# Layer norm of the convolution module: later weight splits, one more row sum on TensorE, and two edits of emission order

## The chip, the cores and the metric

The kernel runs on one core of a Trainium2 chip. The metric is the device time of one execution in microseconds (us); the time of a kernel is the median over its runs. The kernel before takes 2760.52 us, the median of three runs from 2760.06 to 2764.99. The engines are called PE (TensorE), DVE (VectorE), ACT (ScalarE), POOL (GpSimd) and SP (SyncE, which here only issues transfers).

## The reference, cut to what matters

One inference step of a decoder trunk with two layers. The first begins with a Conformer convolution module over 1074 token columns (1040 prompt columns with 16 learned tokens and a little padding, 32 sample columns) of width 1024:

```
def conv_module(x, prefix, w_pw1, b_pw1, w_dw, b_dw, ln_g, ln_b, w_pw2, b_pw2):
    a, g = jnp.split(x @ w_pw1 + b_pw1, 2, axis=-1)
    u = a * jax.nn.sigmoid(g)
    y, tail = causal_dwconv(u, prefix, w_dw)          # 31 taps
    y = jax.nn.silu(layer_norm(y + b_dw, ln_g, ln_b))
    return y @ w_pw2 + b_pw2, tail
```

All matrix products are wanted at float32 accuracy. After this module come a convolutional feed-forward layer, latent attention for the prompt and for eight sample sequences that read a paged cache, and a second feed-forward layer. Only the end of the convolution module and the layer norm behind it are touched by the change.

## The kernel before, in words

Activations lie transposed: the 1024 features are eight tiles of 128 partitions, and a tile has 1074 columns (T0). A float32 operand is split into a high part, rounded by ACT (`split`, L135), and a low part, the rest, by DVE or POOL (L136); a product is three matmuls (high by high, high by low, low by high).

The convolution module (`conv_phase`) goes over the eight feature tiles, c = 0 to 7. Each iteration makes both halves of the first product for its tile (the gemm at L419, with the gate at L402 and L403), then the 31-tap convolution (`conv31`), which leaves the tile y. The taps are multiply-adds on DVE (L523). For the last tile, c = 7, one of the three partial convolutions is done by PE instead: sixteen diagonal matrices of 128 by 128, written by ACT (L395) into two buffers of the pool of raw weights (name `raw`), are multiplied with the shifted sums (L532). A running sum of the tiles y, `total`, is kept by POOL (L446) for the mean of the layer norm.

Between these steps the kernel works off an independent list of pieces, the norms of the cached keys (`cache_norms`): three matmuls into a PSUM tile `pk` (L654), then squares by ACT, either as one square `sq` (L658) which POOL adds up pairwise (L663), or as eight small ones `qq` with an accumulator each (L669). `pk` has two buffers.

`layer_norm` does the following in turn. PE sums `total` and the last tile over the features with a matrix of ones (L573); that is mu. ACT copies it to `m` (L580). DVE subtracts it from tiles 0 to 5 (L585), POOL from tiles 6 and 7 (L583). ACT squares each tile (L589, into buffers named `xl`). The squares of tiles 0, 1 and 2 go to PE directly; those of tiles 4 to 7 are first added on DVE into that of tile 3 (L593). PE makes the sums of the rows, nine matmuls of two columns for each operand that it is given (`add_rows`, L300; the trace counts each of these float32 matmuls as two records). Then DVE computes the reciprocal root (L255 to L260) and PE and ACT spread it over the partitions (L268 to L274). The tiles are scaled (L458), go through SiLU (L460) and are split, and the second product `pw2` begins: the gemm of L175, whose first two weight tiles are loaded and split beforehand (`ahead`, through `weight`, L156).

Each engine works strictly in its own order of instructions. That order is not the order of the code: a scheduler places every instruction by its own estimate of times, with priorities (`high_priority`), except where `manual_schedule` fixes PE's or SP's order. `follow(late, early)` ties one instruction behind another in the order, without a wait. The pool `wp` holds two buffers each for `raw`, `wh` and `wl`; a transfer into a `raw` buffer has to wait until the last reader of that buffer is done, and which of the two buffers a load gets is decided together with the order. All these loads are issued by SP, in order.

Of the kernel before, what the change touches and what calls it, by code (L numbers as in the profile page):

```python
# [9 lines left out]
F32 = mybir.dt.float32  # L10
# [63 lines left out]
HALVE = 16  # L74
HEADS = (0, 1, 2, 3)
SUBS = (6, 7)
# [42 lines left out]
class Prog:  # L119
# [214 lines left out]
    def conv_phase(self):  # L334
# [3 lines left out]
        with ExitStack() as es:  # L338
# [44 lines left out]
            for c in range(KD):  # L383
# [6 lines left out]
                if c == KD - 1:  # L390
                    for half in range(2):
                        d = self.wp.tile([128, 1024], F32, name="raw")
                        for j in range(8):
                            diag.append(d[:, 128 * j:128 * j + 128])
                            nc.scalar.activation(diag[-1], self.cst("ident"), AF.Copy, scale=wsum[:, c, 8 * half + j:8 * half + j + 1])  # L395

# [14 lines left out]
                else:  # L411
                    ch, cnt = T0 // 3, 0
                    for t in range(3):
                        ps = [p.tile([128, 1, 512], F32, name="g")[:, :, :ch] for p in (ga, gg)]
                        with self.manual():
                            for w, p in zip(ws, ps):
                                for k in range(KD):
                                    for i, (x, m) in enumerate(((w[0], xh), (w[0], xl), (w[1], xh))):
                                        y = nc.tensor.matmul(p[:, 0], x[:, k * 128:(k + 1) * 128], m[k][:, t * ch:t * ch + ch],  # L419
                                                             start=k == 0 and i == 0, stop=k == KD - 1 and i == 2)  # L420
                                        self.follow(y, self.wedge)
                                        self.wedge = []
                                        cnt += 1
                                        if EVERY and cnt % EVERY == EVERY // 2:
                                            next(self.fill, None)
                        self.wedge = [y]
                        glu(*ps, t)
# [3 lines left out]
                with self.tc.high_priority(PRIO):  # L431
# [12 lines left out]
                    nc.gpsimd.memset(y[:, 0:2], 0.0)  # L444
                    if 0 < c < KD - 1:
                        nc.gpsimd.tensor_tensor(out=total, in0=total if c > 1 else ys[0], in1=y, op=ALU.add)  # L446
                ys.append(y)
# [20 lines left out]
            self.help = 0  # L468
            ahead = [self.weight(a["pw2"][ot], 1024) for ot in range(2)]
            with self.manual():  # L470
# [94 lines left out]
    def layer_norm(self, ys, total):  # L565
# [12 lines left out]
        with self.tc.high_priority(PRIO):  # L578
# [8 lines left out]
            for k in range(KD):  # L587
# [4 lines left out]
                else:  # L592
                    nc.vector.tensor_tensor(out=qs[-1], in0=qs[-1], in1=q, op=ALU.add)  # L593
            self.add_rows(t, qs, T0)
        self.groups(FILL2)
# [1296 lines left out]
```

## Time and profile before

| | before |
|---|---|
| median of three runs | 2760.52 us (2760.06 to 2764.99) |
| the profiled execution, its own time | 2764.3 us |
| its span, first to last instruction | 2762.4 us |
| mean granted TensorE clock | 0.981 of full |
| PE busy | 2652.8 us, 96% of the span |
| DVE, ACT, POOL busy | 1878.0, 1356.2, 711.0 us |

A row of the timeline gives the start in us, the length, the engine, the line, the operation with the tile written and the tiles read, the shape and the count; in brackets stands how long the engine sat idle before it and what ended the wait. Several equal instructions in a row are merged into one row. Lines are those of the kernel before.

### The profile page before, as it was taken

What the parts mean: (1) busy time and instruction counts of PE and PEld (TensorE: products, weight loads), DVE (VectorE), ACT (ScalarE), POOL (GpSimd) and SP (SyncE); (2) the same over time, 40 slices, a digit from 0 to 9 for tenths busy, and PEclk for the clock granted to TensorE, in tenths of its full rate; (3) what the DMA queues carried; (4) which work ended last, traced back from release to release, by engine and by line L of the source; (5) the groups of instructions that cost most, each with busy time, mean ns of one, the idle gap of its engine ahead of it and who ended that gap; (6) DMA issues with size and microseconds to landing.
All of it is one profiled execution on the core that took longest, in us unless ns stands there. A gap on an engine that the chain in (4) does not pass through costs nothing.

```text
span 2762.4 us, 46569 instructions
## 1 busy us (share of the span) xinstructions
PE 2652.8 (96%) x16966; PEld 2448.0 (89%) x16966; DVE 1878.0 (68%) x3485; ACT 1356.2 (49%) x3701; POOL 711.0 (26%) x1019
## 2 busy tenths in 40 slices
PE   7999997999999999999889999999999999999999
PEld 6888876999999999999767776667999999999999
DVE  8899986578888875135677767676377777775232
ACT  6777775345444553023555555566245454453010
POOL 1567663024333330001111212110023333330000
PEclk9999997999999999999989999999999999999999
DMA  4211101502322236123100001267402222227122
GB/s 142 57 41 55 39 29 42 173 32 87 95 88 94 80 105 238 47 81 107 35 11 18 26 24 32 80 199 261 152 24 89 80 77 85 80 97 244 41 87 76
DMA packets 127769, 238.24 MB, mean 86 GB/s; under 512 B 39778, under 2 KB 81140, under 8 KB 127412
## 3 DMA queue, kind: packets, MB, share of 16 engines
q1 hardware_dynamic: 103828, 200.82, 22.6%
q0 software_dynamic: 9600, 32.36, 3.1%
q10 hardware_dynamic: 14112, 2.09, 0.5%
q8 instruction: 133, 2.18, 0.3%
q14 instruction: 96, 0.79, 0.1%
HBM read 183.90 MB, written 51.31 MB: 85 GB/s over the span
## 4 chain that ended last, share of the span: by engine, by line
PE 85%; DVE 6%; ACT 5%; DMA 2%; issue 2%; POOL 0%; SPq 0%; ACTq 0%; DVEq 0%; POOLq 0%
PE ps L796 30%; PE ps L175 22%; PE pk L654 5%; PE v L1337 5%; PE g L419 4%; PE ps L845 3%; PE p L151 2%; PE ps L197 2%; PE ps L1013 1%; PE po L1651 1%; PE p L1347 1%; PE p L1350 1%; PE p L1349 1%; PE s L1307 1%; PE sn L151 1%
## 5 line engine op out<-in xcount | busy, mean ns | idle before, releaser
L135 ACT ACTIVATE wh<-raw 128x512 fp32r<-128x512 f32 (+2 forms) x256 | 191.1, 749 | 542.0 <-PE ps L175 338.5
L136 DVE TENSOR_TENSOR wl<-raw,wh 128x512 fp32r<-128x512 f32 (+2 forms) x244 | 201.5, 829 | 111.4 <-ACT wh L135 109.2
L942 DVE TENSOR_TENSOR x<-ps,x 128x1074 f32<-128x1074 f32 (+1 forms) x48 | 61.0, 1270 | 293.1 <-PE ps L175 293.1
L766 DVE SCALAR_TENSOR_TENSOR c<-ub,c,c 128x1040 f32<-128x1040 f32 (+1 forms) x176 | 225.1, 1312 | 28.6 <-ACT c L763 27.6
L761 POOL COPY sb<-ub 128x32 f32<-128x32 f32 x88 | 88.8, 1011 | 400.9 <-DVE ub L807 363.2
L669 ACT ACTIVATE qq<-pk 128x64 f32<-128x64 f32 x736 | 158.1, 243 | 67.6 <-PE pk L654 67.5
L1337 PE MATMUL v<-pf,vf 128*128 128x512 f32 (+4 forms) x448 | 176.6, 478 | 10.0 <-ACT pf L1354 9.7
L663 POOL TENSOR_TENSOR sq<-sq 128x256 f32<-128x256 f32 (+4 forms) x229 | 140.2, 623 | 102.6 <-ACT sq L658 95.6
L175 PE MATMUL ps<-xh,wh 128*128 128x358 f32 (+1 forms) x672 | 148.3, 329 | 9.1 <-ACT xh L135 5.9
L1354 ACT ACTIVATE pf<-p 128x512 f32<-128x512 f32 (+4 forms) x224 | 99.0, 451 | 118.1 <-DVE p L1352 98.1
L669 ACT ACTIVATION_READ_ACCUMULATOR qq<-pk 128x1 f32 x736 | 153.9, 227 | 0.0
L523 DVE SCALAR_TENSOR_TENSOR a<-u,c,a 128x512 f32<-128x512 f32 x216 | 150.1, 745 | 4.9 <-ACT a L516 4.9
L175 PE MATMUL ps<-xh,wl 128*128 128x358 f32 (+1 forms) x672 | 147.6, 328 | 0.0
L175 PE MATMUL ps<-xl,wh 128*128 128x358 f32 (+1 forms) x672 | 147.4, 327 | 0.1
L175 PE MATMUL ps<-al,wh 128*128 128x358 f32 (+1 forms) x672 | 147.2, 327 | 0.0
L175 PE MATMUL ps<-ah,wl 128*128 128x358 f32 (+1 forms) x672 | 146.5, 326 | 0.0
L175 PE MATMUL ps<-ah,wh 128*128 128x358 f32 (+1 forms) x672 | 146.2, 326 | 0.0
L654 PE MATMUL pk<-ukh,ch 128*128 128x512 f32 x256 | 115.5, 452 | 25.6 <-ACT ch L135 13.4
L763 ACT ACTIVATE c<-ub,c 128x1074 f32<-128x1074 f32 (+1 forms) x88 | 101.3, 1185 | 59.7 <-DVE ub L807 46.8
L175 PEld LDWEIGHTS ps<-xh,wh 128*128 128x128 f32 x672 | 117.5, 191 | 12.7 <-ACT xh L135 6.8
L658 ACT ACTIVATE sq<-pk 128x512 f32<-128x512 f32 x164 | 99.8, 613 | 50.8 <-PE pk L654 48.5
L135 ACT ACTIVATE wh<-s 128x512 fp32r<-128x512 f32 x120 | 75.7, 631 | 94.9 <-PE ps L796 88.3
(599 smaller groups left out, 9100.4 us busy)
## 6 DMA issues: line engine op xcount, KB each, us to landing
raw<-wup SPq DMA_DIRECT2D x88, 512.0 KB, 3.5
pg<-ctn SPq DMA_DIRECT2D x128, 192.0 KB, 3.8
raw<-wdn SPq DMA_DIRECT2D x32, 448.0 KB, 3.3
raw<-pw SPq DMA_DIRECT2D x24, 512.0 KB, 3.9
d_a<-c POOLq DMA_DIRECT2D x22, 537.0 KB, 3.5
raw<-d_a SPq DMA_DIRECT2D x22, 537.0 KB, 5.2
d_a<-c POOLq DMA_DIRECT2D x22, 531.0 KB, 3.1
raw<-d_a SPq DMA_DIRECT2D x22, 531.0 KB, 5.3
```

Source lines behind the costliest of these rows:

```text
L135: return (nc.scalar.activation(h, src, AF.Copy), (eng or nc.vector).tensor_tensor(out=l, in0=src, in1=h.bitcast(F32), op=ALU.subtract))
L136: (eng or nc.vector).tensor_tensor(out=l, in0=src, in1=h.bitcast(F32), op=ALU.subtract))
L175: nc.tensor.matmul(p[:, c, :ch], s[:, k * 128:(k + 1) * 128], m[k][:, off + c * ch:off + (c + 1) * ch], start=k == 0 and i == 0, stop=k == ...
L419: y = nc.tensor.matmul(p[:, 0], x[:, k * 128:(k + 1) * 128], m[k][:, t * ch:t * ch + ch], start=k == 0 and i == 0, stop=k == KD - 1 and i ...
L523: nc.vector.scalar_tensor_tensor(out=p[:, :ND] if j == n - 1 else acc, in0=x[:, j:j + ND], scalar=w[:, j:j + 1], in1=to if j == 1 else acc ...
L654: x = nc.tensor.matmul(ps, s[:, j, :], m[:, 512 * c:512 * c + 512], start=i == 0, stop=i == 2)
L663: nc.gpsimd.tensor_tensor(out=to, in0=v[:, :, :n], in1=v[:, :, n:2 * n], op=ALU.add)
L669: nc.scalar.activation(q, ps[:, 64 * h:64 * h + 64], AF.Square, accum_out=ss[:, p, 8 * c + h:8 * c + h + 1])
L763: x = nc.scalar.activation(c, ub, AF.Copy, scale=wd[:, t, 2:3])
L766: nc.vector.scalar_tensor_tensor(out=c[:, 2:pe], in0=ub[:, tap:tap + pe - 2], scalar=wd[:, t, tap:tap + 1], in1=c[:, 2:pe], op0=ALU.mult, ...
L796: nc.tensor.matmul(ps, w[:, s], m[:, lo:hi], start=first and k == 0 and i == 0, stop=k == KD // 2 - 1 and i == 2, skip_group_check=True)
L1337: nc.tensor.matmul(o[:, at_:], vf[:m, b, c], p[:m, :512 - at_], start=b == 0, stop=last)
```

## The change

Four edits. The diagonal matrices of tile 7 are no longer emitted in a block ahead of the gemm but one at each of the points in the gemm's loop where a piece of the cache work is emitted. The running sum adds a tile one iteration later (`ys[c - 1]` in iteration c), outside the priority block. The low parts of the first two `pw2` weights are tied behind `self.summed`, the last addition of squares on DVE. And the square of tile 7 is given to PE as an operand of its own instead of being added on DVE: five operands go to the row sums instead of four, in the order 0, 1, 2, 7, 3.

```
-HEADS = (0, 1, 2, 3)
+HEADS = (0, 1, 2, 3, 7)
...
-                    for half in range(2):
-                        d = self.wp.tile([128, 1024], F32, name="raw")
-                        for j in range(8):
-                            diag.append(d[:, 128 * j:128 * j + 128])
-                            nc.scalar.activation(diag[-1], self.cst("ident"), AF.Copy, scale=wsum[:, c, 8 * half + j:8 * half + j + 1])
+                    ds = [self.wp.tile([128, 1024], F32, name="raw") for _ in range(2)]
+                    diag = [ds[j // 8][:, 128 * (j % 8):128 * (j % 8) + 128] for j in range(16)]
+                made = 0
...
                                             next(self.fill, None)
+                                            if made < len(diag):
+                                                nc.scalar.activation(diag[made], self.cst("ident"), AF.Copy, scale=wsum[:, c, made:made + 1])
+                                                made += 1
...
-                    if 0 < c < KD - 1:
-                        nc.gpsimd.tensor_tensor(out=total, in0=total if c > 1 else ys[0], in1=y, op=ALU.add)
+                if c > 1:
+                    nc.gpsimd.tensor_tensor(out=total, in0=total if c > 2 else ys[0], in1=ys[c - 1], op=ALU.add)
...
-            ahead = [self.weight(a["pw2"][ot], 1024) for ot in range(2)]
+            ahead = []
+            for ot in range(2):
+                ahead.append(self.weight(a["pw2"][ot], 1024))
+                self.follow(self.last[1], [self.summed])
...
-                    nc.vector.tensor_tensor(out=qs[-1], in0=qs[-1], in1=q, op=ALU.add)
-            self.add_rows(t, qs, T0)
+                    self.summed = nc.vector.tensor_tensor(out=qs[3], in0=qs[3], in1=q, op=ALU.add)
+            self.add_rows(t, [qs[i] for i in (0, 1, 2, 4, 3)], T0)
```

What this makes of the engines' orders is shown at three places, all between the end of tile 7's convolution and the row sums. The number behind a name tells buffers apart.

SP, the loads of the second product's weights. `raw_6233` of before and `raw_6241` of the change hold the first `pw2` tile, `raw_6239` and `raw_6247` the second, the other two the third and fourth; in brackets are the engines that a transfer waits for. Before:

```order
L156 DMA raw_6233<-pw2 128x1024 [waits DMAHW7_49,PE_49]
...
L156 DMA raw_6239<-pw2 128x1024 [waits DMAHW7_49,DMAHW4_49,DVE_49]
L156 DMA raw_6493<-pw2 128x1024 [waits DMAHW5_49,PE_49]
L156 DMA raw_6660<-pw2 128x1024 [waits DMAHW6_49,DMAHW4_49,DVE_49]
L479 DMA xr_6479<-x0 128x1074
```

And in the change:

```order
L156 DMA raw_6241<-pw2 128x1024 [waits DMAHW7_49,PE_49]
...
L156 DMA raw_6247<-pw2 128x1024 [waits DMAHW4_49,PE_49]
L156 DMA raw_6501<-pw2 128x1024 [waits DMAHW5_49,DMAHW7_49,DVE_49,Activation_49]
L156 DMA raw_6668<-pw2 128x1024 [waits DMAHW4_49,DMAHW6_49,DVE_49,Activation_49]
L483 DMA xr_6487<-x0 128x1074
```

The second weight tile went, before, into the buffer of the first one, once DVE had made that one's low part; now it goes into the other buffer, whose last reader is PE's sixteenth diagonal matmul.

DVE, from the last taps of tile 7 to the reciprocal root (`x7` is the tile that `conv31` finishes, `xl3` the sum of squares). Before:

```order
L136 TENSOR_TENSOR wl_6236<-raw_6233,wh_6235 128x1024
L523 SCALAR_TENSOR_TENSOR fa_5675<-u_5067,c1_58,a1_5919 128x512
...
L541 TENSOR_TENSOR x7_5674<-g_5678,fa_5675 128x512
L542 TENSOR_TENSOR x7_5674<-fb_5676,fa_5675 128x8
L136 TENSOR_TENSOR wl_6242<-raw_6239,wh_6241 128x1024
L585 SCALAR_TENSOR_TENSOR x0_939<-ps_5982,x0_939 128x1074
...
L593 TENSOR_TENSOR xl3_6050<-xl3_6050,xl6_6058 128x1074
L593 TENSOR_TENSOR xl3_6050<-xl3_6050,xl7_6061 128x1074
L255 TENSOR_SCALAR nr_v_6152<-ps_6033 128x9
```

And in the change:

```order
L527 SCALAR_TENSOR_TENSOR fa_5674<-u_5066,c1_58,a1_5918 128x512
...
L546 TENSOR_TENSOR x7_5673<-fb_5675,fa_5674 128x8
L545 TENSOR_TENSOR x7_5673<-g_5677,fa_5674 128x512
L589 SCALAR_TENSOR_TENSOR x0_939<-ps_5982,x0_939 128x1074
...
L597 TENSOR_TENSOR xl3_6050<-xl3_6050,xl6_6058 128x1074
L136 TENSOR_TENSOR wl_6244<-raw_6241,wh_6243 128x1024
L136 TENSOR_TENSOR wl_6250<-raw_6247,wh_6249 128x1024
L255 TENSOR_SCALAR nr_v_6160<-ps_6033 128x9
```

Both low parts moved behind the additions, and the fourth addition is gone.

ACT, from the second weight's high part to the squares (`qq` and `sq` belong to the cache work, `xl0` is the square of tile 0). Before:

```order
L135 ACTIVATE wh_6241<-raw_6239 128x1024
L669 ACTIVATE qq_6013,ss_135<-pk_6009 128x64
...
L658 ACTIVATE sq_6107<-pk_6103 128x512
L580 ACTIVATE m_6034<-ps_5982 128x1074
L658 ACTIVATE sq_6119<-pk_6115 128x512
L658 ACTIVATE sq_6131<-pk_6127 128x512
L589 ACTIVATE xl0_6044<-x0_939 128x1074
L658 ACTIVATE sq_6143<-pk_6139 128x512
L589 ACTIVATE xl1_6046<-x1_1612 128x1074
L589 ACTIVATE xl6_6058<-x6_4982 128x1074
L589 ACTIVATE xl2_6048<-x2_2286 128x1074
```

And in the change:

```order
L135 ACTIVATE wh_6249<-raw_6247 128x1024
L673 ACTIVATE qq_6013,ss_135<-pk_6009 128x64
...
L584 ACTIVATE m_6034<-ps_5982 128x1074
L662 ACTIVATE sq_6115<-pk_6111 128x512
L662 ACTIVATE sq_6127<-pk_6123 128x512
L593 ACTIVATE xl0_6044<-x0_939 128x1074
L662 ACTIVATE sq_6139<-pk_6135 128x512
L662 ACTIVATE sq_6151<-pk_6147 128x512
L593 ACTIVATE xl6_6058<-x6_4981 128x1074
L593 ACTIVATE xl1_6046<-x1_1612 128x1074
L593 ACTIVATE xl2_6048<-x2_2285 128x1074
```

The copy `m` stands ahead of one more square of the cache work, two such squares instead of one follow `xl0`, and tile 6's square comes before tile 1's. The second weight's high part and the eight `qq` stand ahead of `m` in both.

On PE the row sums of the square of tile 7 (nine matmuls) stand between those of tiles 2 and 3; the three matmuls of the last tile's mean (L573) follow each other, where before a piece of the cache work stood between the second and the third. ACT's diagonal matrices and POOL's running sums stand at the same places among their engines' instructions as before. Further back the scheduler also exchanged instructions in three later stages: the latents (about 1350 to 1400 us), the attention of the samples (about 1830 to 1910 us), where splits of cache pages (`ch`, `kh`) stand ahead of copies and exponentials which they followed, and the start of the output projection.

## Rows read from the trace of the kernel before

**Rows 1.** The head of the page: span, and each engine's busy time, share of the span and instructions.

```profile
span 2762.4 us, 46569 instructions
PE 2652.8 (96%) x16966; PEld 2448.0 (89%) x16966; DVE 1878.0 (68%) x3485; ACT 1356.2 (49%) x3701; POOL 711.0 (26%) x1019
```

**Rows 2.** The chain that ended last, in the stretch from 402 to 457 us: start, length, what.

```profile
402.51 10.61 DVE a L523 x17
...
414.37 1.13 DVE wl L136
...
426.84 5.94 ACT xl L589 x6
...
432.80 2.33 DVE xl L593
...
435.22 1.35 DVE xl L593
...
439.34 4.02 PE ps L300 x18
```

**Rows 3.** The timeline of PE in the same stretch.

```profile
412.89 4.45 PE L532 MATMUL g<-fb,raw 128*128 128x512 f32 x10
...
420.04 1.47 PE L573 MATMUL ps<-x,ones 128*128 128x358 f32 x4 [0.19 <-DVE x L541]
...
422.04 0.76 PE L573 MATMUL ps<-x,ones 128*128 128x358 f32 x2
...
426.41 9.15 PE L300 MATMUL ps<-ones,xl 128*128 128x2 f32 x54 [0.98 <-ACT xl L589]
439.34 4.00 PE L300 MATMUL ps<-ones,xl 128*128 128x2 f32 x18 [3.78 <-DVE xl L593]
...
455.49 1.26 PE L175 MATMUL ps<-xh,wh 128*128 128x358 f32 x3 [5.38 <-ACT xh L135]
```

**Rows 4.** The timeline of ACT there.

```profile
419.07 1.06 ACT L135 ACTIVATE wh<-raw 128x1024 fp32r<-128x1024 f32 x1 [4.50 <-DMA raw<-pw]
...
421.51 0.25 ACT L669 ACTIVATION_READ_ACCUMULATOR qq<-pk 128x1 f32 x1
...
422.84 1.07 ACT L580 ACTIVATE m<-ps 128x1074 f32<-128x1074 f32 x1
...
425.25 1.10 ACT L589 ACTIVATE xl<-x 128x1074 f32<-128x1074 f32 x1 [0.37 <-DVE x L585]
426.26 0.58 ACT L658 ACTIVATE sq<-pk 128x512 f32<-128x512 f32 x1
426.74 7.02 ACT L589 ACTIVATE xl<-x 128x1074 f32<-128x1074 f32 x7
```

**Rows 5.** SP's issues from 385 to 500 us, and how long the loads of `raw` took from issue to landing between 405 and 430 us.

```profile
415.52 6.22 SPq L156 DMA_DIRECT2D raw<-pw  x3
...
486.68 0.33 SPq L484 DMA_DIRECT2D d_r<-x  x1
...
DMA to landing us min/median/max: 3.5/3.7/4.3
```

**Rows 6.** The timeline of DVE there: the two low parts of weights, and the instruction that completes tile 7.

```profile
414.28 1.21 DVE L136 TENSOR_TENSOR wl<-raw,wh 128x1024 fp32r<-128x1024 f32 x1
...
419.29 0.69 DVE L541 TENSOR_TENSOR x<-g,fa 128x512 f32<-128x512 f32 x1
...
420.16 1.23 DVE L136 TENSOR_TENSOR wl<-raw,wh 128x1024 fp32r<-128x1024 f32 x1
```

**Rows 7.** Stretches of the span: from and to, length, busy time of each engine with instructions begun, granted TensorE clock (1.00 is 2.4 GHz, 0.50 is 1.2 GHz), DMA share, GB/s.

```profile
426.00:431.00 5.00, 4.59 (x34) 4.59 (x34) 5.00 (x5) 5.00 (x7) 5.00 (x6) 0.82 0.22 88
431.00:436.00 5.00, 4.56 (x22) 4.47 (x21) 3.23 (x3) 2.76 (x3) 5.00 (x12) 0.50 0.00 0
...
456.00:460.00 4.00, 3.95 (x14) 3.48 (x13) 4.00 (x4) 3.97 (x5) 0.00 (x0) 0.51 0.00 0
460.00:465.00 5.00, 5.00 (x30) 4.78 (x29) 5.00 (x6) 4.97 (x6) 0.00 (x0) 1.00 0.00 0
```

**Rows 8.** The same view for the row sums (L300) alone: length, PE busy and records, weight loads, granted clock.

```profile
426.40:429.40 3.00, 2.99 (x26) 2.99 (x27) 0.97 0.22 90
429.40:432.40 3.00, 3.00 (x15) 3.00 (x16) 0.50 0.02 5
```

**Rows 9.** The timeline of POOL there.

```profile
424.22 4.93 POOL L583 TENSOR_TENSOR x<-x,m 128x1074 f32<-128x1074 f32 x2
...
433.87 1.31 POOL L663 TENSOR_TENSOR ss<-sq 128x8 f32<-128x8 f32 x1
```

**Rows 10.** Single lines: the diagonal matrices on ACT and the running sum on POOL. Least, median and longest duration in ns, first and last start.

```profile
L395 ACT ACTIVATE raw<-c,wsum x16: 396/413/427, 339.3 to 352.2; 128x128 f32<-128x128 f32 x16
...
L446 POOL TENSOR_TENSOR total<-total,x x5: 2488/2507/2515, 216.3 to 388.3; 128x1074 f32<-128x1074 f32 x5
```

**Rows 11.** Two later stretches in the view of rows 7: the latents, and the attention of the samples.

```profile
1350.00:1400.00 50.00, 35.73 (x186) 30.45 (x185) 43.17 (x154) 33.13 (x94) 13.69 (x19) 0.86 0.16 46
1830.00:1910.00 80.00, 74.71 (x448) 57.28 (x448) 58.23 (x122) 57.77 (x136) 10.84 (x20) 0.96 0.85 278
```

**Rows 12.** Waits between 1830 and 1935 us: who waited for whom, us in total, times, longest.

```profile
ACT ch L135 <- DMA pg<-ctn: 9.7, 8, 2.5
...
PEld sn L151 <- ACT ch L135: 1.8, 4, 0.8
```

## The prediction, made before the change was run

> **What bounds the kernel now.** I read the head of the page first: PE is busy for 2652.8 of 2762.4 us [rows 1], so a change can give at most the 110 us in which PE waits, and what it gives must come from a place where the chain of waits leaves PE. The end of tile 7's convolution and the layer norm behind it is such a place. The chain there goes through DVE's taps and the first low part of a weight (1.13 us at 414.37), the squares on ACT, four additions on DVE and the last eighteen records of the row sums [rows 2]. The reader is to see in PE's timeline that PE waits for the additions before those records (3.78 us), and again for the first split tile before the second product begins at 455.49 [rows 3]. Then I read who stands in front of whom on each engine: ACT [rows 4], SP [rows 5], DVE [rows 6]; and last the granted clock, which falls to half inside the row sums and is full again only after 460 [rows 7, 8].
>
> **The change part by part.**
>
> *Diagonal matrices and running sum.* The sixteen diagonal matrices and the running sums stand at the same places in ACT's and POOL's order as before (the part on the change says so), with the durations of [rows 10]. I cost both edits at nothing; nothing has to hide them, because nothing moved.
>
> *Low part of the first weight out of DVE's taps.* DVE gets to the instruction that completes tile 7 1.13 us earlier [rows 2], at about 418.2 instead of 419.29 [rows 6] (a short one of the sample columns now goes before it). PE takes the tile at about 419.7, when its cache matmuls are done, instead of 420.04, and does the six L573 records without the cache piece that split them (before: four from 420.04, two from 422.04, end 422.80 [rows 3]). At four records in about 1.0 us they end near 421.5. So mu is ready 1.2 us earlier. That is what this edit offers.
>
> *The load of the second weight.* What is late next is ACT. Ahead of the copy m stands the second weight's high part, which began at 419.07 after 4.50 us of waiting for its load [rows 4]. That load was issued at 415.52 [rows 5], the moment the first low part ended on DVE (414.28 + 1.21 [rows 6]), and took 3.55 us to the start on ACT. By the order of the change it waits instead for the sixteenth diagonal matmul, which ends at 412.89 + 4.45 = 417.34 [rows 3]. With the same 3.55 us (landings took 3.5 to 4.3 [rows 5]) the high part begins at 420.9. From its start to the end of the eight small squares ACT needed 2.5 us (419.07 to 421.51, plus 0.1 for the last to pass [rows 4]), and m comes right behind: 423.4 instead of 422.84. So m is 0.6 us later, not 1.2 earlier. If the load landed as late as 4.3 it would be 1.3 later; were it in time, m would be bound by PE, 1.2 earlier. I take +0.6: the row is the same load on the same queue.
>
> *The order of the squares.* Tile 0's square follows m as before, so at 425.85 (425.25 + 0.6). Tile 1's began 1.49 us after it (426.74 − 425.25 [rows 4]). Now one more cache square (426.26 to 426.74, 0.48) and the square of tile 6 (5.94/6 = 0.99 [rows 2]) stand in between. POOL can have tile 6 ready: its subtraction takes 2.5 us (4.93/2 [rows 9]) from m's end at 424.5 to 427.0, and ACT's turn is at 427.8. Tile 1's square begins at 428.8 and ends (1.1 us) at 429.9, tile 4's begins at 428.8 + 4 × 0.99 = 432.8 and ends at 433.9.
>
> *One addition less, eighteen records more.* DVE makes three additions: 2.33 + 1.35 + 1.35 = 5.0 us [rows 2] from 433.9, done at 438.9, before PE has come to them. PE does 90 records instead of 72. Tile 0's eighteen go from 427.0 at full clock (26 records in 2.99 us, 0.115 each [rows 8]) to 429.1; then PE waits for tile 1 until 429.9. The other 72 follow without a gap, at half clock: 3.00/15 = 0.20 each [rows 8], or, with the ends of the runs, (9.15 + 4.00 − 2.99)/46 = 0.22 [rows 3]. With 0.21 they take 15.1 and PE ends at 445.0, against 443.34. That is +1.7. If the clock stays full for the first few records of tile 1 it is +1.0; if the new gaps in front (PE waits for ACT to release cache tiles behind m) make it fall before tile 0, tile 0's records take 3.7 us instead of 2.1 and it is +2.5. I take +1.6. So the addition that is removed (1.35) buys nothing: its place on the path is taken by 18 records at half clock (3.7 us), which just fill the 3.78 us wait.
>
> *The low parts behind the additions.* 2 × 1.22 us [rows 6] from 438.9 to 441.4 on DVE, in front of the reciprocal root, which waits for PE until 445.0. They cost nothing; without that cover they would cost 2.4. The third and fourth weight loads on SP now wait for them, 20 us later than before, and the two loads of the residual wait behind those; the next issue on SP was at 486.68 [rows 5] and the gemm that uses them comes after it, so 45 us of cover remain. POOL is not asked for anything by then.
>
> One rule of the Trainium skill bears on this: SBUF — State Buffer, section on the two separate sides, says that DVE and GpSimd share a pair of ports as an exclusive lock, which a DVE operation with two SBUF inputs takes against a GpSimd operation that reads SBUF, and that the loser blocks wholly. The trace agrees as far as it goes: the first addition took 2.33 us and the next 1.35 [rows 2], while POOL's small sum beside it took 1.31 [rows 9]. By the rule all five DVE operations could be held up like the first, to 3 × 2.33 + 2 × 2.2 = 11.4 us from 433.9; they would end at 445.3, 0.3 us behind PE's 445.0, and the sum would be +1.9.
>
> *Everything behind.* From the end of the row sums to the first matmul of the second product the orders are the same for the tiles that PE waits for (12.15 us from 443.34 to 455.49 [rows 3]), so the delay passes on in full, and PE's own work behind it takes it to the end.
>
> *Exchanged instructions in later stages.* In the latents PE was idle for 14.3 of 50 us, in the samples for 5.3 of 80 [rows 11]. The best that another order could do there is to remove the 5.3, and a part of the 14.3 that the rows don't bound well, since DVE is busy for 43.2 of the 50. The worst in the samples is that all of ACT's waits for cache pages, 9.7 us in eight, reach PE; so far 1.8 us of waits behind ACT's page splits did [rows 12]. The order puts more page splits ahead of copies, which speaks for a loss, but PE was at 93%, with matmuls of several pieces interleaved. I take 0 and keep −5 and +8 as ends.
>
> **The sum.** The profiled execution took 2764.3 us on a span of 2762.4, 1.9 around it. With +1.6 the span would be 2764.0 and the execution 2765.9. That execution lies 3.8 us above the median of the runs shown; on the median, 2760.5 + 1.6 = 2762.1 us.
>
> **The rivals.**
>
> *The first weight's low part really was the bound* and the gain reaches PE. For it speaks the chain of waits, which has it as a link. Against it stands the load above. Even with the load in time, m at 421.6, tile 1's square would end at 428.1, the 72 records at 443.2, and the gain would be 0.1: 2760.4.
>
> *The clock stays full* because PE no longer waits in front of the last records. Then the last eighteen start when DVE is done (438.9) and end near 441.3, 2.0 us early; the second product's first 4 us, at 0.51 before [rows 7], would gain 2.0, and the nine transposes between them 0.7: about 2755.8. Against it: the clock went to half while the first 54 records ran back to back [rows 3, 7, 8], so it was not the wait that took it away.
>
> The rule beside this is in the Trainium skill, TensorE: Matmul & The Clock Gate, Part 1: "the default state is throttled, and activity releases the throttle". That speaks for this rival where added records count as activity; the fall within unbroken records speaks for the other side.
>
> *Page splits block ACT in the samples' attention.* ACT takes its instructions in order; a split that now stands ahead of a copy or an exponential holds these back while its page is still on the way. Price: up to 2.5 us for each such wait [rows 12], at three places where the order moved a pair ahead, 7.5 us less what PE has in hand. It decides from about 4 us on: 2760.5 + 1.6 + 4 = 2766 or more, up to 2769.6.
>
> *The latents' new order is better*, by a wait or two of PE, some 3 us: 2759.
>
> **How the numbers follow.** Forecast (layer norm +1.0 to +2.5, the rest within 2 us) 0.55; gain absorbed, no change 0.13; full clock 0.07; blocked page splits 0.13; better order in a later stage 0.12. What a measurement of this kernel can tell from no change is about 0.2%, 5.5 us, the spread of its three runs. Under 2755.0 lies half of the full-clock case, a small part of the better orders and the scatter of the runs: 0.11. Over 2766.0 lie most of the blocked splits and a few runs of the forecast: 0.16. In between: 0.73. The range is 2756 to 2769: the forecast with its bounds and the runs' scatter of some 3 us to either side, on the low side up to the full clock, on the high side most of the blocked splits.
>
> **What would show it.** Right: in the changed profile ACT waits for the load of raw until about 420.9 and m starts near 423.4; the row sums are 90 records with one short gap after the first eighteen, at half clock, ending near 445; DVE waits for PE before the reciprocal root; the low parts lie in that wait. Wrong: a high part that begins before 420, a granted clock of 1.00 between 431 and 436, or a first matmul of the second product before 455.5. A total that differs by more than 3 us from the shift of that first matmul would show that a later stage decided.

## The result, and the profile after

The change runs in 2769.59 us, the median of seven runs (2765.34 to 2775.21), beside 2762.47 us for the kernel before on the same chip (seven runs, 2757.38 to 2769.95): ratio 1.003, 95% interval 1.0018 to 1.0042. It is slower by 7 us between the medians and by 8 by the ratio, whose interval reaches from 5 to 12. The forecast was 2762.1, in a range to 2769. Two of the missing 7.5 us are the base: the three runs it was reckoned from had a median of 2760.5. Most of the rest is a step that I had put at 0.

The profiled execution of the change took 2770.76 us on a span of 2768.7. The head of its page, as [rows 1]:

```profile
span 2768.7 us, 46603 instructions
PE 2658.7 (96%) x16984; PEld 2455.0 (89%) x16984; DVE 1876.7 (68%) x3484; ACT 1356.1 (49%) x3701; POOL 707.1 (26%) x1019
```

PE has 18 more instructions, and is busy for 5.9 us more. 18 records at half clock are 3.7 us of that, so something else stretches PE's work too.

**The layer norm.** ACT's timeline there, as [rows 4] (lines 135, 584 and 593 are before's 135, 580 and 589), and after it PE's, as [rows 3]:

```profile
420.60 1.06 ACT L135 ACTIVATE wh<-raw 128x1024 fp32r<-128x1024 f32 x1 [6.48 <-DMA raw<-pw]
423.14 1.12 ACT L584 ACTIVATE m<-ps 128x1074 f32<-128x1074 f32 x1
425.60 1.10 ACT L593 ACTIVATE xl<-x 128x1074 f32<-128x1074 f32 x1 [0.37 <-DVE x L589]
```

```profile
412.53 4.45 PE L536 MATMUL g<-fb,raw 128*128 128x512 f32 x10
...
419.33 1.97 PE L577 MATMUL ps<-x,ones 128*128 128x358 f32 x6
...
423.35 0.51 PE L658 MATMUL pk<-ukh,ch 128*128 128x512 f32 x1 [1.35 <-ACT qq L673]
...
424.79 0.80 PE L658 MATMUL pk<-ukh,ch 128*128 128x512 f32 x1 [0.47 <-ACT sq L662]
425.38 0.63 PE L658 MATMUL pk<-ukh,cl 128*128 128x512 f32 x1
...
427.52 2.31 PE L300 MATMUL ps<-ones,xl 128*128 128x2 f32 x18
430.45 14.64 PE L300 MATMUL ps<-ones,xl 128*128 128x2 f32 x72 [0.61 <-ACT xl L593]
457.23 1.26 PE L175 MATMUL ps<-xh,wh 128*128 128x358 f32 x3 [5.38 <-ACT xh L135]
```

The reader is to see that the last tile's mean is ready early (six records from 419.33), but that ACT sits 6.48 us in front of the second weight's high part, and PE waits twice for ACT behind it. From the second of these waits on the cache matmuls take 0.63 us instead of 0.40. The granted clock, as [rows 7], says the same, and that it was full again during tile 0's row sums (the 18 records from 427.52) and at half once more for nearly all of the 72 that follow:

```profile
424.80:427.50 2.70, 2.70 (x6) 2.17 (x7) 2.70 (x3) 2.01 (x3) 2.70 (x2) 0.50 0.00 0
428.20:431.00 2.80, 2.19 (x20) 2.10 (x20) 2.80 (x3) 2.80 (x4) 2.80 (x4) 1.00 0.00 0
432.00:445.00 13.00, 13.00 (x62) 13.00 (x61) 6.50 (x5) 3.33 (x4) 10.07 (x21) 0.50 0.30 94
```

Counted from the ten diagonal matmuls to the second product, the stage takes 44.70 us (457.23 − 412.53) against 42.60 in [rows 3]. DVE's rows, as [rows 2, 6], and SP's, as [rows 5]:

```profile
434.38 4.30 DVE L597 TENSOR_TENSOR xl<-xl,xl 128x1074 f32<-128x1074 f32 x3 [2.89 <-ACT xl L593]
438.59 2.42 DVE L136 TENSOR_TENSOR wl<-raw,wh 128x1024 fp32r<-128x1024 f32 x2
445.13 0.17 DVE L255 TENSOR_SCALAR nr_v<-ps 128x9 f32<-128x9 f32 x1 [4.11 <-PE ps L300]
```

```profile
417.01 24.41 SPq L156 DMA_DIRECT2D raw<-pw  x3
```

The low parts lie in DVE's wait for PE, and the two loads behind them are issued only when they are done, by 441.4.

**The end of the samples.** The other place is 1500 us later. PE's timeline of the change (lines 1644, 1655 and 1667 are before's 1640, 1651 and 1663), and ACT's beside it:

```profile
1907.27 0.30 PE L1644 MATMUL pp<-c,s 128*64 128x128 f32 x1
1907.99 0.65 PE L1655 MATMUL po<-cn,pt__23298 64*64 64x128 f32 x4 [0.42 <-ACT pt__23298 L1646]
1909.41 0.36 PE L1667 MATMUL pp<-c,ob 64*128 64x64 f32 x1 [0.78 <-ACT ob L1666]
1910.12 1.97 PE L1644 MATMUL pp<-c,s 128*128 128x128 f32 x8 [0.34 <-ACT s L1633]
...
1912.32 3.67 PE L1655 MATMUL po<-pg,pt__23329 128*64 128x128 f32 x16
```

```profile
1907.66 0.27 ACT L1646 ACTIVATE pt__23298<-pp 64x128 f32<-64x128 f32 x1 [5.38 <-PE pp L1644]
...
1918.37 1.06 ACT L135 ACTIVATE xh<-x 128x1030 fp32r<-128x1030 f32 x1
```

And PE and ACT of before at the same work:

```profile
1901.60 0.27 PE L1640 MATMUL pp<-c,s 128*64 128x128 f32 x1
...
1907.40 1.97 PE L1640 MATMUL pp<-c,s 128*128 128x128 f32 x8 [1.01 <-ACT s L1629]
1909.30 2.58 PE L1651 MATMUL po<-pg,pt__23321 128*64 128x128 f32 x16
```

```profile
1914.12 1.06 ACT L135 ACTIVATE xh<-x 128x1030 fp32r<-128x1030 f32 x1
```

In before PE makes the last, 64-column transpose of the samples' third pair at 1901.60, with seven matmuls of scores and 16 value matmuls behind it to fill the time until ACT has copied it (`pt`). In the change it stands behind those 16 matmuls, at 1907.27. ACT has waited 5.38 us for it, and the exponentials of the fourth pair, which PE needs next, stand behind that copy. PE stops three times (0.42, 0.78, 0.34) where before it stopped once (1.01), and the next 16 value matmuls take 3.67 us instead of 2.58. By five-microsecond stretches, in the view of [rows 7], before and then the change:

```profile
1905.00:1910.00 5.00, 3.99 (x21) 3.20 (x21) 1.29 (x7) 3.83 (x12) 0.00 (x0) 0.72 1.02 409
1910.00:1915.00 5.00, 5.00 (x39) 4.32 (x39) 0.32 (x2) 3.28 (x9) 0.00 (x0) 0.94 0.88 337
...
1930.00:1935.00 5.00, 5.00 (x32) 5.00 (x32) 3.29 (x10) 2.52 (x10) 0.00 (x0) 1.00 0.77 246
```

```profile
1905.00:1910.00 5.00, 3.58 (x26) 2.79 (x26) 2.40 (x9) 2.31 (x7) 0.00 (x0) 0.94 1.00 384
1910.00:1915.00 5.00, 4.88 (x22) 4.43 (x23) 0.55 (x2) 3.80 (x12) 0.00 (x0) 0.50 0.93 370
...
1930.00:1935.00 5.00, 5.00 (x22) 5.00 (x22) 1.67 (x2) 2.58 (x4) 0.00 (x0) 0.50 0.54 155
```

The clock column says 0.50 twice in the change, at 1910 and again at 1930, inside the output projection, where PE is busy for the whole 5 us but begins 22 matmuls instead of 32. Before's own dip in the first of these stretches (0.72) is over sooner.

### The profile page after: what moved, and what is told of

It reads as the page before. It is cut to its first block, busy times and chain, and to the rows that moved or that the text cites. A ratio compares the mean times of both kernels' runs of the same rounds, so it can differ in the third digit from the quotient of the medians.

```text
span 2768.7 us, 46603 instructions
## 1 busy us (share of the span) xinstructions
PE 2658.7 (96%) x16984; PEld 2455.0 (89%) x16984; DVE 1876.7 (68%) x3484; ACT 1356.1 (49%) x3701; POOL 707.1 (26%) x1019
## 4 chain that ended last, share of the span: by engine, by line
PE 85%; DVE 6%; ACT 4%; DMA 2%; issue 2%; POOL 0%; SPq 0%; ACTq 0%; DVEq 0%
PE ps L800 30%; PE ps L175 22%; PE pk L658 5%; PE g L417 4%; PE v L1341 4%; PE ps L849 3%; PE p L151 2%; PE ps L197 2%; PE ps L1017 1%; PE p L1351 1%; PE p L1353 1%; PE p L1354 1%; PE s L1311 1%; PE po L1655 1%; PE sn L151 1%
```

## The experiments

Theory A: the change loses 2 to 3 us in the layer norm, and 5 or more because the scheduler, fed with other times, exchanged instructions in the samples and the projection. Rivals: B, the delay itself shifts everything behind it against the page transfers, whatever the order; C, the layer norm is all, and the rest is scatter between two profiles. The kernel before was timed again with each group of runs; its medians were 2759.57, 2762.09 and 2760.23 us. The groups ran on different chips, so kernels of different groups are compared by their ratios to before.

**The change, with before's order behind the latents.** Multiplications by 1.0 of a 128x9 tile on DVE are enough to make the scheduler decide otherwise:

```
+            for _ in range(3):
+                nc.vector.tensor_scalar(out=r9, in0=r9, scalar1=1.0, scalar2=None, op0=ALU.mult)
             norms(0, p[0])
```

> The change, with three multiplications by 1.0 of a 128x9 tile on DVE added in the latents (some 0.2 us). They make the scheduler emit the samples' attention and the output projection in the order of the kernel before; up to the latents the order is the change's. Theory A (the exchanged order of the samples' attention and of the projection costs about 5 us; the layer norm costs about 2): this kernel is 2 us above before, ratio 1.0007, at most 1.0012, and 5 us under the change. Theory B (the delay of the layer norm shifts everything behind it against the page transfers, whatever the order): it stays at the change's ratio, 1.003. Theory C (the change's loss is the layer norm alone, and the rest is scatter between profiles): 1.0007 too, but then the second kernel of this job is at 1.000.

Measured: 2763.61 us against 2759.57, ratio 1.0008 (0.9998 to 1.0019), the number of theories A and C; B falls. The change's own layer norm is in it (45.98 us in its profile).

**Before, with the change's order of the samples.** The same edit, four times, in before.

> The kernel before, with four such multiplications on DVE in the latents, which make the scheduler emit the samples' attention in the change's order (the projection too but for two matmuls). The convolution module and the layer norm are those of before. Theory A: 5 us above before, ratio 1.0018 (1.0012 to 1.0026). Theories B and C: within 1 us of before, ratio 1.000.

Measured: 2771.62 us, ratio 1.0039 (1.0024 to 1.0054). It is more than A expected, and not all of it is the samples: the four multiplications also moved the latents, and from their first matmul (L1013) to the first of L1277 this profile took 97.9 us against 91.2 in before. With that, the time alone doesn't decide against C. What speaks against C here is the end of the samples with the projection, 123.4 us as in the change (123.5) against 117.7 in before; the tail of the samples is the change's to the tenth (17.1 us, table below). And the change's loss is no scatter: the kernel with the third and fourth edit alone, below, repeats it (1.0031).

**Three edits, without the fifth operand.** `HEADS` and the order of the operands as before.

> The change without its fourth edit: diagonals one by one, running sum a tile later and tied low parts, but four operands for the row sums as before. The samples and the projection are in the order of before. By the working of the prediction m is 0.6 us later, tile 4's square ends at 433.9, four additions end at 440.4, the last eighteen records near 444.4 against 443.34: the layer norm costs 1.0 us. Theory A: ratio 1.0004 (1.0000 to 1.0009). Theory B: 1.002 or more, since half of the delay is there.

Measured: 2763.50 us, ratio 1.0008 (0.9998 to 1.0019). The stage took 44.35 us, 1.8 more than in before's profile where I had 1.0: the 54 records, which took 9.15 us in [rows 3], took 11.51, since the clock fell already in the cache matmuls in front.

**The fifth operand alone.**

```
-HEADS = (0, 1, 2, 3)
+HEADS = (0, 1, 2, 3, 7)
```

(and the operands in the change's order)

> Before with the fourth edit alone: 90 row-sum records and three additions, the low parts of both weights still among DVE's taps. The samples and the projection are in the order of before. By the rows of before the first 72 records run to about 439.3 and the last 18 need not wait for the additions (438.0), so the sums end at 443.1 against 443.34: the layer norm costs 0. Theory A: ratio 1.000 (0.9995 to 1.0007). Theory B: 1.000. If records at half clock cost more than I took, 1.0005 to 1.001.

Measured: 2762.56 us, ratio 1.0010 (1.0000 to 1.0019); the stage took 43.56 us, 90 records in 17.53 us without a gap. I had expected no loss. I had reckoned from before's profile, in which the four additions took 6.49 us and PE waited 3.78 us for them [rows 3]; in the four other profiles with four additions and the second load in its old place they took 5.4 to 5.6 us, and the stage 41.70 to 42.16. Against those the fifth operand costs 1.4 to 1.9 us. See the last section.

**One tie in the samples.** To see which exchange costs, the 64-column transposes are put back ahead of the value matmuls in the change, for the third pair alone (`held` are the first value matmuls of the group before):

```
+                if sp == 2 and new:
+                    for x in held:
+                        self.follow(x, [y])
```

> The change with one tie: in the samples' third pair the value matmuls of the last page group stand behind the 64-column transposes on PE, as in before; the samples' order up to there stays the change's, the projection's start changes a little. In the profiles with the change's order (the change, and the second run of the first job) ACT waited 5.4 us there for those transposes with the next pair's exponentials behind it, PE idled in three pieces, and from the last scores to the end of the samples it took 17.1 us; with before's order 13.3 to 14.6. Theory D (this one inversion is the price in the samples, and the half clock behind it that in the projection): the stretch is back at 14.5, the time at 1.0008 to 1.0015 of before. Theory E (other exchanges, page splits above all, cost it): 1.0025 to 1.003.

Measured: 2769.05 us against 2762.09, ratio 1.0022 (1.0011 to 1.0033). The ratio lies between the two theories' numbers, and its interval covers both. The tail fell from 17.1 to 15.2 us, but the tie moved the start of the projection, and there PE now waits for a weight's split:

```profile
1921.14 0.43 PE L151 MATMUL ps<-xh,wh 128*128 128x354 f32 x1 [0.67 <-ACT wh L135]
1922.40 0.66 PE L151 MATMUL ps<-xh,wl 128*128 128x354 f32 x1 [0.66 <-DVE wl L136]
```

**A third order.** One multiplication instead of three, in the change.

> The change with one multiplication by 1.0 in the latents instead of three: it gives a third order of the samples, with page splits and copies exchanged at other places than before's and the change's, and of the projection's start; the tail of the third pair is as in before. Theory D: 1.0008 (1.0000 to 1.0016). Theory E (any exchange of page splits ahead of copies costs): 1.002 to 1.004.

Measured: 2769.46 us, ratio 1.0029 (1.0020 to 1.0039). The number is E's; theory D, that the one inversion in the tail is the whole price, falls. But the loss is not where E had it, since the samples proper took 104.5 us, less than in before: here the tail is good (13.3 us) and the projection is not (108.0 us against 101.8 to 103.3 in seven of eight profiles with before's order). PE waits there eight times, among them

```profile
1920.01 0.43 PE L151 MATMUL ps<-xh,wh 128*128 128x354 f32 x1 [1.26 <-ACT wh L135]
...
1931.57 0.43 PE L151 MATMUL ps<-xl,wh 128*128 128x354 f32 x1 [0.84 <-DVE xl L136]
```

where in before only two waits (0.28 and 0.51) are left after the samples.

**The third and fourth edit; the first and second.** Two kernels, each with half of the diff.

> The third and fourth edit alone (tied low parts, square of tile 7), without the diagonals and the running sum: every engine's order is the change's but for eight diagonals' and some additions' places. If the first two edits cost nothing, as predicted, this kernel is at the change's ratio, 1.003 to 1.004. If they cost (or gain) something, it differs from that by more than 0.001.

Measured: 2770.05 us, ratio 1.0031 (1.0020 to 1.0043): the change's ratio.

> The first two edits alone: diagonals one by one and the running sum a tile later. Nothing moves in any engine's order but a few small additions on POOL. Predicted 1.000 (0.9993 to 1.0007). A rival that puts a part of the loss here says 1.001 or more.

Measured: 2757.99 us, ratio 0.9993 (0.9983 to 1.0003). The first two edits cost nothing that can be told from no change.

**The inversion alone, in before.** The reverse of the tie above: `self.follow(y, [held])`, with `y` the 64-column transposes and `held` the last value matmul of the group before.

> The kernel before with one tie: in the samples' third pair the 64-column transposes on PE stand behind the value matmuls of the last page group, as in the change. Everything ahead of that point is word for word before's order; ACT's splits for the projection move a little behind it. If the inversion alone makes the loss of the samples' tail and of the projection, the stretch from the last scores to the first d_x gemm of the second feed-forward layer grows from about 117 us by 3 to 6 and the ratio is 1.001 to 1.002. If the inversion costs only its own waits: 1.5 to 2.5 us, 1.0005 to 1.001. If the loss is in the projection's order: 1.000.

Measured: 2764.11 us against 2760.23, ratio 1.0011 (1.0002 to 1.0021). The tail took 16.8 us and the projection 105.3. ACT's `ob` stands behind the copy, two splits and two exponentials, and PE pays for it:

```profile
1911.83 0.27 PE L1665 MATMUL pp<-c,ob 64*128 64x64 f32 x1 [2.19 <-ACT ob L1664]
```

By the ratio the inversion costs some 3 us by itself (0.6 to 6 by the interval), at the low end of the first of the three branches, and half of the 0.0022 that lie between the change and the change with before's order. Its waits are not those of the change, and the profiled execution (2771.41 us) was the slowest of the kernel's twelve, so the 16.8 and 105.3 may be long for it.

**Which tie lengthens the layer norm.** `self.follow(self.last[1], [self.summed])` for one `ot` only, in before.

> Before with the tie for the second weight's low part alone. The second load goes into the same buffer as in before and waits for DVE's first low part, as in before. Load theory (the tied low part of the FIRST weight makes the layer norm longer, since it gives the second load PE's sixteenth diagonal to wait for): ACT's second high part starts 3.5 to 4.3 us after the load's issue, about 4.8 us after the ten last diagonal matmuls begin, or some 6.2 us after them in before's profile; the stretch from these matmuls to the second product is 41.7 to 42.6, as in before. Rival (any low part placed behind the additions lengthens it): 44 or more.

> Before with the tie for the first weight's low part alone. The second load goes into the other buffer and waits for PE's sixteenth diagonal. Load theory: ACT's second high part starts some 8 us after the ten last diagonal matmuls begin (8.07 in the change's profile), PE waits in front of the cache matmuls, the clock falls before the row sums begin, and the stretch to the second product is 44 to 44.7, as with both ties (44.35). Rival (it takes both ties, or the low parts' place on DVE): 42.6 or less.

Measured: 2757.76 and 2764.17 us, one run each. ACT's high part and PE's first row sums, with the second low part tied and then with the first:

```profile
418.65 1.06 ACT L135 ACTIVATE wh<-raw 128x1024 fp32r<-128x1024 f32 x1 [4.37 <-DMA raw<-pw]
...
426.04 9.79 PE L300 MATMUL ps<-ones,xl 128*128 128x2 f32 x54 [0.99 <-ACT xl L593]
```

```profile
421.57 1.06 ACT L135 ACTIVATE wh<-raw 128x1024 fp32r<-128x1024 f32 x1 [6.29 <-DMA raw<-pw]
...
428.34 11.51 PE L300 MATMUL ps<-ones,xl 128*128 128x2 f32 x54
```

Their ten diagonal matmuls begin at 412.52 and 413.49, so the high part starts 6.13 and 8.08 us after them, and the stage takes 41.70 and 44.57 us. The load theory holds: it is the first weight's low part, by the buffer that the second load then gets.

**The change with the second tie alone.** Its scheduler happens to leave the samples and the projection in before's order.

> The change with the tie for the second weight's low part alone. The second load is in before's place, and the scheduler leaves the samples and the projection in before's order. Load theory and theory A together: the stretch of the layer norm is that of the fourth edit alone, about 43.6, and the ratio 1.0005 (0.9995 to 1.001). If the layer norm's loss is in the fifth operand and the additions rather than in the load: 1.001.

Measured: 2761.89 us, ratio 1.0003 (0.9989 to 1.0017); stage 43.72 us. The stage is as theory A and the load theory have it together. The ratio's interval doesn't exclude the other branch's 1.001.

The stretches of all profiles side by side, in us. Layer norm: from the ten diagonal matmuls to the second product. Samples: from the first L1601 to the last L1610 (lines of before). Tail: from there to the last L1663. Projection: from there to the last matmul of its closing gemm (L197). All are differences of start times in one profiled execution each. Those of "change, late restored" (2770.17 us; median 2763.61) and of "before, late transposes" (2771.41; median 2764.11) were the slowest executions of their kernels:

```
                         order behind   layer   samples   tail   projection   ratio
before                   before's       42.60   106.0     14.4   103.3        1
diagonals and sum        before's       41.86   106.7     13.3   101.8        0.9993
second low part          before's       41.70   105.7     14.8   101.8        (one run)
first low part           before's       44.57   104.7     14.8   101.8        (one run)
no fifth operand         before's       44.35   109.3     14.4   103.3        1.0008
fifth operand alone      before's       43.56   108.3     14.6   101.9        1.0010
change, second tie       before's       43.72   106.5     14.6   101.8        1.0003
change, late restored    before's       45.98   106.6     13.3   108.7        1.0008
the change               the change's   44.70   108.7     17.1   106.4        1.0030
tie and square           the change's   44.49   106.8     16.2   104.4        1.0031
before, late only        the change's   41.72   107.4     17.1   106.3        1.0039
change, tail tie         tied           44.58   107.0     15.2   105.3        1.0022
change, third order      third          44.41   104.5     13.3   108.0        1.0029
before, late transposes  tied           42.16   105.4     16.8   105.3        1.0011
```

## Why the prediction was wrong, and where it was right

**The step that failed** is "Exchanged instructions in later stages", where I wrote "I take 0 and keep −5 and +8 as ends". The exchange costs some 6 us. In time it is what lies between the change (1.0030, or 1.0031 without the first two edits) and the same layer norm with the old order behind it (1.0008): 0.0022. The intervals of the two leave some 2 to 10 us, by my estimate. The profiles agree: tail and projection together take 123.5, 120.6 and 123.4 us in the three with the change's order, and 115.1 to 117.7 in seven of the eight with before's. The eighth, 122.0, is a slow execution of the change with before's order restored. There ACT waited for a transfer, PE behind it, and the clock fell to half, so a long projection comes with before's order too; the kernel's median lies 6.6 us below that execution:

```profile
1922.48 1.06 ACT L135 ACTIVATE xh<-x 128x1030 fp32r<-128x1030 f32 x1 [0.78 <-DMA x<-d_o]
1923.60 0.43 PE L151 MATMUL ps<-xh,wh 128*128 128x354 f32 x1 [0.86 <-ACT xh L135]
```

I looked at the right stages with the wrong question. I asked whether ACT's waits for pages would reach PE, and bounded them by the sum of ACT's waits [rows 12]. The samples proper, where pages are waited for, are no longer with the change's order (106.8 to 108.7 us) than with before's (104.7 to 109.3). The change's profile does show a wait of PE of 1.53 us behind a page split at 1857.98, and half clock after it, but the fifth operand alone, with before's order, shows the like (1.12 us at 1859.05, clock 0.66 between 1860 and 1870).

The loss lies behind them, in the hand-over between PE and ACT at the end of the samples and in the projection. In the tail the change has three waits, and some 7 us at half clock (from about 1909.7 to 1916.5). In the projection its waits are no more than before's (0.52 us against 0.28 and 0.51), and the 3 us more come with the half clock from about 1930 on; the tie and the square alone, with the clock full there, have four waits (0.52, 0.96, 0.32 and 0.34), and the third order has eight. So the place is shown, and not one mechanism for all of it.

The trace of before would have told the danger in the tail: PE already waits there for ACT (1.01 us in front of the last pair, and two short waits behind it), so whatever the new order delays in ACT's queue comes out on PE. The part on the change names the exchange of the output projection; the working gave it no term. The sign that I had set for this case came: the total moved by 7 us and the first matmul of the second product by 2.1 in its stage, more than 3 apart.

**The rival "page splits block ACT in the samples' attention"** had the place nearly right and the size right (2766 to 2769.6, chance 0.13), but not the mechanism.

**The layer norm** went nearly as forecast: m at 423.14 and row sums ending near 445.1, both from a start 0.36 earlier; counted from before's start that is 423.5 (forecast 423.4) and 445.45 (445.0); DVE's low parts in the wait. The load of the second weight took away what the first low part gave, as worked out, and the runs with one tie each show it. The term was +1.6; it measured +2.1 between the two profiles, and +2.7 between the medians of the five profiles with both ties and the fifth operand (44.58) and of the five with four operands and the second load in its old place (41.86). Two things were mis-sized. The cache matmuls behind the new waits ran at half clock (0.63 us each), which moved the squares behind them by 0.9. And before's profile was long in this stage: 42.60, where its four like took 41.70 to 42.16. That the sum came so near is in part luck, for its parts don't add up: beside the median of 41.86, the fifth operand alone gives 43.56 and 43.72, the moved load alone 44.35 and 44.57, and both together 44.58. I had written 0 and +1.0 for the two alone.

**The clock.** The rival in which it stays full did not happen. In the change it fell twice in the layer norm: at 424.8 among cache matmuls, behind two waits of PE (1.35 and 0.47), and, after it had been full from 428.2 to 431, again near 431.5, within 72 records without a gap, as it had within the 54 of before [rows 8]. So the bound of +2.5, which let it fall ahead of tile 0's records, had the fall right and its length wrong: these took 2.31 us, not 3.7. The rule I had set beside the rival (the Trainium skill, TensorE: Matmul & The Clock Gate, Part 1: "the default state is throttled, and activity releases the throttle") agrees so far as the fall at 424.8 and the one near 1909.7 (among waits of 0.42, 0.78 and 0.34) came with waits of PE. It doesn't tell of the falls within records without a gap, nor of that near 1930. There the change fell to 0.50 behind one wait of 0.52 us, and before, behind waits of 0.28 and 0.51, did not; but "before, late only" in the table, behind the same 0.28 and 0.51, did. Both kernels that fell there with the change's order had been at half clock from 1910 to 1915 too; the change with before's order restored (0.53 and 0.50 from 1925 to 1935) had not. Why stays open.

**Diagonals and running sum at nothing**: right (0.9993). **"Everything behind passes on in full"**: the delay was still 2.0 us at 627 us, and could not be told from the scatter of the profiles at 1304 (−0.55).

What is not settled: how the 6 us divide between the tail and the projection, since each attempt to put one back moved the other, and whether the exchange in the latents has a part in them (91.2 us in before's profile and 92.8 in the change's, but 94.4 in that of the inversion alone, where before's order stands). The inversion in the tail alone is worth 3 us in before (1.0011), and taking it back is worth 2 in the change (1.0022 against 1.0030), with intervals as wide as that.

## What to carry to other kernels

Where a scheduler orders the program, a local edit is judged in two parts: its own stage, and the order that falls out behind it; a few tiny instructions, or a tie, can hold one part still while the other is measured. Look for exchanges first where two engines hand work back and forth with little between them: a copy that moves behind sixteen matmuls on one engine holds everything that stands behind it on the other. And of a deferred read ask which buffer it keeps: here a low part that nobody was waiting for moved the next load behind another engine's work, and with it the stage.

## What the runs showed of the hardware

DVE and POOL slow each other in the additions of squares, and who loses changes from profile to profile. In before's profile DVE's four additions took 6.49 us, of which the first took 2.33 [rows 2]; in the profile with the change's late order and before's layer norm they took 5.61, and POOL's series of twelve was the one that stretched. In order, before and that kernel, DVE and then POOL:

```profile
432.80 6.49 DVE L593 TENSOR_TENSOR xl<-xl,xl 128x1074 f32<-128x1074 f32 x4 [1.66 <-ACT xl L589]
429.08 4.86 POOL L663 TENSOR_TENSOR sq<-sq 128x64 f32<-128x64 f32 x12
```

```profile
431.64 5.61 DVE L593 TENSOR_TENSOR xl<-xl,xl 128x1074 f32<-128x1074 f32 x4 [1.66 <-ACT xl L589]
427.94 8.09 POOL L663 TENSOR_TENSOR sq<-sq 128x64 f32<-128x64 f32 x12
```

The first addition lasted 2.3 to 2.7 us in six of the fourteen profiles and 1.3 to 1.6 in the other eight, and POOL's small sums beside the additions that didn't lose lasted 1.2 to 1.5 us, where their neighbours took 0.2 to 0.5.

The rule of the Trainium skill that the prediction weighed (SBUF — State Buffer, section on the two separate sides: a shared pair of ports as an exclusive lock, whose loser blocks) fits the exchange of roles and the length of those sums, but not the sum of 11.4 us that I worked out from it: in the change DVE's five operations took 4.30 and 2.42 us beside a POOL that was busy from 429.22 to 441.40.
